# Attention heads: scores from two-term keys and queries, probabilities turned in place

## The chip, the cores and the metric

The kernel runs on one core of a Trainium2 chip. The metric is the device time of one execution in microseconds; the median of three runs counts. TensorE (PE in the profile) multiplies matrices, VectorE (DVE) and ScalarE (ACT) work element by element, GpSimd (POOL) issues most of the small transfers (DMAs), SyncE (SP) the loads of the weights. Each engine works through its own instructions in order and waits on semaphores for the others.

## The reference

One decoder layer on 512 tokens of width 2048, all in float32. What the change touches is the forgetting attention, 8 heads of 128:

```
c = cumsum(log_sigmoid(f_logit + b_f))           # per head, over tokens
logits = q @ k.T * 128**-0.5 + c[:, None] - c[None, :]
logits = where(causal, logits, -inf)
p = softmax(logits)                              # 512 x 512, lower triangle
attn = p @ v
```

Before it stands one input projection (conv B, C, V, Q, K, V, forget logits, gates); behind it gated sums, an output projection and a squared-ReLU MLP.

## The kernel before

Large products are fp32r products of two terms: a value is split into a high part (`high_of`, a rounding copy on ACT, L111) and a low part (`low_of`, a subtraction on DVE, L114), and high x high, high x low and low x high are added in PSUM (L171, L175, L177). A 512x512 block product is done as seven products of quarters (a Strassen scheme, `Group`), whose operand sums are DVE subtractions of 128x2048 (L128). One quarter product is 32 + 16 products of 256 columns. The weight quarters are loaded into four buffers `x`, their parts into two buffers each, `th` and `tl`.

The attention heads have no stage of their own. They run between the products of the first four conv groups (the input projection's columns for the convolution): `beat` counts these products, and at counts held in `places` a step of a head is put between them: `meet(h)` at 76 + 156 h (mix of head h-1, fetch of its values, scores of head h), `shares` 52 later, `turn_of(h)` 112 later. On TensorE these steps keep the order in which they are written (`sure`); on the other engines a list scheduler sets the order from its own estimates.

A head's steps: `terms` fetches a row of the running sums into the first 512 columns of `p` in all partitions; `values` fetches the values `vv`; `scores` puts a mask into PSUM (a bf16 identity times a bf16 mask, L911), adds fp32 products of queries and keys (L916), reduces each of the four row blocks with the terms into `p` (DVE, L929, which also finds the extreme of each row) and takes exponentials (ACT, L935); `shares` divides by the row sums (L941, L944); `turns` transposes ten 128x128 blocks on TensorE (L952) and copies them to `pT` (DVE L954, L955, ACT L956); `mixed` multiplies them with the values (L963, ten fp32 products of 128 columns), copies the sums to `pT` (ACT, L965) and stores them to `a_d` (POOL, L966). Row block qi holds (qi+1) x 128 columns; in `p` it begins at column 896, 1024, 512, 0 for qi = 0 to 3 (`AT`). Each of `p`, `pT`, `vv`, `kT` and `qT` has one buffer.

Of the kernel before, what the change touches and what calls it, by code (L numbers as in the profile page):

```python
# [24 lines left out]
NH = AW // P  # L25
DFF = 4 * D
EPS = 1e-6
NEG = -1.0e30
# [17 lines left out]
def tile_hybrid_block(ctx: ExitStack, tc, x, g_mix, w_in, b_f, b_gate, conv_w, w_conv_out,  # L46
                      w_attn_out, w_mix_out, g_mlp, w_ff1, w_ff2, g_final, out):
    nc = tc.nc
    x, out = x[0], out[0]
# [3 lines left out]
    const = ctx.enter_context(tc.tile_pool(name="const", bufs=1))  # L53
# [9 lines left out]
    def bank(i, name):  # L63
        return psum.tile([P, S], F32, tag=f"p{i}", name=name)
# [51 lines left out]
    def split(src, hi, lo):  # L116
        return high_of(src, hi), low_of(src, hi, lo)
# [426 lines left out]
    class Quarters:  # L544
# [162 lines left out]
    both = pair(6, F32, "junk")  # L707
# [131 lines left out]
    def at(tag, name=None, shape=None, bufs=1):  # L839
        return pb.tile(shape or [P, S], F32, tag=tag, name=name or tag, bufs=bufs)  # L840
# [7 lines left out]
    nc.vector.scalar_tensor_tensor(out=lf, in0=fl, scalar=0.0, in1=fa, op0=ALU.min, op1=ALU.subtract)  # L848
    AT = (P * 7, P * 8, P * 4, 0)
    BANK = ((7, 3 * P), (6, 0), (7, 0), (5, 0))  # L850

    def rows_of(tag, name, w=1280):
        return at(tag, name, [P, 1280])[:, :w]

    raw_ut = rows_of("pT", "ut", S)
# [3 lines left out]
    ut = pb.tile([P, 1280], F32R, tag="p", name="utr")[:, :S]  # L859
    nc.scalar.activation(out=ut, in_=raw_ut, func=AF.Copy)  # L860
    lf2 = pb.tile([P, 2, NT, NH], F32R, tag="vv", name="lf2")
    lf2 = lf2[:, 0], lf2[:, 1]
    split(lf, *lf2)
    identb = const.tile([P, P], BF16, name="identb")
    nc.vector.tensor_copy(identb, ident)
    maskb = const.tile([P, P], BF16, name="maskb")
    nc.gpsimd.memset(maskb, 0.0)
    nc.gpsimd.affine_select(out=maskb, in_=maskb, compare_op=ALU.is_ge, fill=NEG, base=0,
                            pattern=[[-1, P]], channel_multiplier=1)
    cn = const.tile([P, NT, NH], F32, name="cn")  # L870

    def sure(i):
        return tc.keep_in_program_order(i)

    def running():

        pc = bank(4, "pc")
        for t in range(NT):
            for e in range(2):
                sure(nc.tensor.matmul(pc[:NH, t * P:], lf2[e][:, t, :], ut[:, :S - t * P], start=(t == 0 and e == 0),  # L880
                                      stop=(t == NT - 1 and e == 1)))
        ncT = at("pT", "ncT", [P, 1280])[:NH, :S]
        nc.vector.tensor_scalar(out=ncT, in0=pc[:NH, :], scalar1=-1.0, scalar2=None, op0=ALU.mult)
        nc.gpsimd.dma_start(out=c_d, in_=ncT)
        return ncT

    class Head:


        def __init__(self, h):  # L890
            self.h = h
            self.kT, self.qT = at("kT"), at("qT")
            nc.gpsimd.dma_start(out=self.kT, in_=kq_d[0, h])
            nc.gpsimd.dma_start(out=self.qT, in_=kq_d[1, h])

        def terms(self):
            self.p = at("p", shape=[P, 1280])
            nc.gpsimd.dma_start(out=self.p[:, :S], in_=c_d[self.h:self.h + 1, :].to_broadcast([P, S]))

        def values(self):  # L900
# [4 lines left out]
        def scores(self):  # L905
            p, h = self.p, self.h
            at_bank = {i: bank(i, "sc") for i in (7, 6, 5)}
            sc = [at_bank[i][:, c:c + (qi + 1) * P] for qi, (i, c) in enumerate(BANK)]

            def masked(o, n):  # L910
                sure(nc.tensor.matmul(o.rearrange("p (n k) -> p n k", n=n), identb,  # L911
                                      maskb.unsqueeze(1).to_broadcast([P, n, P]), start=True, stop=False,
                                      skip_group_check=True))
# [12 lines left out]
            least, bias, total, back = (stat.tile([P, NT], F32, tag=n, name=n) for n in ("nm", "bias", "sm", "rs"))  # L926
            for qi in range(NT):
                n = (qi + 1) * P
                nc.vector.tensor_tensor_reduce(out=p[:, AT[qi]:AT[qi] + n], in0=sc[qi], in1=p[:, :n], scale=-1.0,  # L929
                                               scalar=-NEG, op0=ALU.add, op1=ALU.min, accum_out=least[:, qi:qi + 1])  # L930
            sub(bias, least, cn[:, :, h])
            add(bias, bias, cn[:, :, h])
            for qi in range(NT):
                o = p[:, AT[qi]:AT[qi] + (qi + 1) * P]
                nc.scalar.activation(out=o, in_=o, func=AF.Exp, bias=bias[:, qi:qi + 1], scale=-1.0,  # L935
                                     accum_out=total[:, qi:qi + 1])
            self.total, self.back = total, back
# [6 lines left out]
                nc.vector.tensor_scalar(out=o, in0=o, scalar1=back[:, qi:qi + 1], scalar2=None, op0=ALU.mult)  # L944

        def turns(self):
            self.pT = at("pT", shape=[P, 1280])
            at_bank = {i: bank(i, "tp") for i in (7, 6, 5)}
            for qi in (0, 2, 1, 3):
                i, c = BANK[qi]  # L950
                for ki in range(qi + 1):
                    sure(nc.tensor.transpose(at_bank[i][:, c + ki * P:c + (ki + 1) * P],  # L952
                                             self.p[:, AT[qi] + ki * P:AT[qi] + (ki + 1) * P], ident))
            nc.vector.tensor_copy(self.pT[:, S:2 * S], at_bank[7])  # L954
            nc.vector.tensor_copy(self.pT[:, 2 * S:], at_bank[6][:, :2 * P])  # L955
            nc.scalar.activation(out=self.pT[:, :S], in_=at_bank[5], func=AF.Copy)  # L956
# [12 lines left out]
    heads8, places = {}, {}  # L969

    def begin_terms():
        ncT = running()
        heads8[0].terms()
        heads8[0].values()

        def columns():
            pcn = bank(5, "pcn")
            for t in range(NT):
                sure(nc.tensor.transpose(pcn[:, t * NH:(t + 1) * NH], ncT[:, t * P:(t + 1) * P], ident[:NH, :NH]))
            nc.vector.tensor_scalar(out=cn.rearrange("p t h -> p (t h)"), in0=pcn[:, :NT * NH], scalar1=-1.0,  # L980
                                    scalar2=None, op0=ALU.mult)
        places[FIRST - 20] = columns

    def meet(h):

        def step():
            if h > 0:
                heads8[h - 1].mixed()
                if h < NH:
                    heads8[h].values()  # L990
            if h < NH:
                heads8[h].scores()
                if h + 1 < NH:
                    heads8[h + 1] = Head(h + 1)
        return step

    def turn_of(h):

        def step():
            heads8[h].turns()  # L1000
            if h + 1 < NH:
                heads8[h + 1].terms()
        return step

    for h in range(NH + 1):
        places[FIRST + PERIOD * h] = meet(h)
        if h < NH:
            places[FIRST + PERIOD * h + SHARE] = lambda h=h: heads8[h].shares()
            places[FIRST + PERIOD * h + TURN] = turn_of(h)
    places[32] = begin_terms  # L1010
    heads8[0] = Head(0)
    made = [0]

    def step_at(n):
# [81 lines left out]
    n = 0  # L1096
# [784 lines left out]
```

## Time and profile before

| | us |
|---|---|
| median of 3 runs | 2405.5 (2404.98 to 2408.44) |
| profiled execution | 2406.2 |
| its span, first to last instruction | 2404.5 |
| PE busy | 2389.2 |
| DVE busy | 2030.0 |
| ACT busy | 1205.1 |

The span is what the core's instructions cover; the execution's time has 1.7 us around it. The views used below: the page's list of engines; a table of stretches; lists of waits; the chain of waits, followed back from the last instruction, each piece being what the next one was released by; timelines of an engine; the transfers with their time from issue to landing. Records of TensorE overlap, since products are pipelined: the pace is read from one start to the next, or from the chain.

### The profile page before, as it was taken

The numbers are of one execution on the slowest core, as the hardware profiler recorded it, in microseconds if no ns is written. First come the engines' busy times: TensorE is split into PE (matmuls) and PEld (weight loads), VectorE is DVE, ScalarE is ACT, GpSimd is POOL, SyncE is SP. The second block draws the span as 40 slices with busy tenths as digits, with TensorE's granted clock in tenths as the row PEclk, the third lists the DMA queues.
The fourth block names the chain that finished last, engine by engine and source line by source line (L and its number), as shares of the span: only waits on it lengthen the run. The fifth ranks groups of instructions, "written<-read, shape, count | busy, mean of one in ns | idle before, by whom it ended". The sixth has DMA issues, their size and how long they took to land.

```text
span 2404.5 us, 41377 instructions
## 1 busy us (share of the span) xinstructions
PE 2389.2 (99%) x17778; PEld 2256.0 (94%) x17778; DVE 2030.0 (84%) x1684; ACT 1205.1 (50%) x1240; POOL 288.2 (12%) x459
## 2 busy tenths in 40 slices
PE   9999999999999999999999999999999999999998
PEld 9999999999999999899999999999998888888886
DVE  7987777789888778889988989888897888889898
ACT  7443444445545534456656666665665333333334
POOL 1100111121111102012200000000001001100000
PEclk9999999999999999999999999999999999999999
DMA  8665544565565756566856565665688557665662
GB/s 277 183 191 154 168 145 150 156 204 159 172 207 177 259 191 209 161 210 223 316 192 231 183 232 181 214 213 197 233 303 293 169 196 253 219 217 183 231 231 101
DMA packets 282599, 491.98 MB, mean 205 GB/s; under 512 B 11820, under 2 KB 192136, under 8 KB 282032
## 3 DMA queue, kind: packets, MB, share of 16 engines
q1 hardware_dynamic: 229552, 277.96, 36.5%
q0 software_dynamic: 50096, 206.39, 23.4%
q10 hardware_dynamic: 2768, 4.99, 0.6%
q8 instruction: 139, 2.28, 0.4%
q14 instruction: 44, 0.36, 0.0%
HBM read 379.70 MB, written 109.07 MB: 203 GB/s over the span
## 4 chain that ended last, share of the span: by engine, by line
PE 91%; issue 3%; DVE 3%; ACT 1%; DMA 1%; POOL 1%; SPq 0%; DVEq 0%; POOLq 0%; ACTq 0%
PE a L171 6%; PE a L175 6%; PE a L177 6%; PE d L171 5%; PE d L175 5%; PE a L199 5%; PE a L197 5%; PE a L195 5%; PE d L177 5%; PE c L171 4%; PE c L177 4%; PE c L175 4%; PE d L195 3%; PE d L197 3%; PE d L199 3%
## 5 line engine op out<-in xcount | busy, mean ns | idle before, releaser
L111 ACT ACTIVATE th<-x 128x2048 fp32r<-128x2048 f32 (+1 forms) x280 | 537.0, 1918 | 479.9 <-DVE x L128 162.7
L114 DVE TENSOR_TENSOR tl<-x,th 128x2048 fp32r<-128x2048 f32 (+2 forms) x282 | 639.3, 2273 | 151.9 <-ACT th L111 147.7
L128 DVE TENSOR_TENSOR x<-x,x 128x2048 f32<-128x2048 f32 (+1 forms) x160 | 365.9, 2287 | 23.0 <-DMA x<-in_w_in_dram 18.4
L111 ACT ACTIVATE th<-y 128x2048 fp32r<-128x2048 f32 (+1 forms) x109 | 185.4, 1701 | 273.2 <-PE a L197 138.8
L114 DVE TENSOR_TENSOR tl<-y,th 128x2048 fp32r<-128x2048 f32 (+1 forms) x109 | 219.3, 2013 | 26.7 <-ACT th L111 26.3
L197 PE MATMUL a<-th,us 128*128 128x512 f32 x512 | 199.2, 389 | 0.0
L195 PE MATMUL a<-th,us 128*128 128x512 f32 x512 | 199.2, 389 | 0.0
L171 PE MATMUL c<-S,th 128*128 128x256 f32 x848 | 195.7, 277 | 0.0
L175 PE MATMUL c<-S,th 128*128 128x256 f32 x848 | 195.5, 276 | 0.0
L171 PE MATMUL a<-S,th 128*128 128x256 f32 x784 | 181.5, 278 | 1.0 <-ACT o L269 1.0
L175 PE MATMUL a<-S,th 128*128 128x256 f32 x784 | 180.3, 276 | 0.0
L175 PEld LDWEIGHTS c<-S,th 128*128 128x128 f32 x848 | 159.3, 188 | 0.0
L171 PEld LDWEIGHTS c<-S,th 128*128 128x128 f32 x848 | 159.3, 188 | 0.0
L171 PEld LDWEIGHTS a<-S,th 128*128 128x128 f32 x784 | 147.2, 188 | 1.4 <-ACT o L269 1.2
L175 PEld LDWEIGHTS a<-S,th 128*128 128x128 f32 x784 | 147.3, 188 | 0.2 <-issue 0.2
L199 PE MATMUL a<-tl,us 128*128 128x512 f32 x512 | 136.7, 389 | 0.0
L171 PE MATMUL a<-A,th 128*128 128x256 f32 x544 | 126.6, 278 | 0.0
L171 PE MATMUL b<-A,th 128*128 128x256 f32 x544 | 126.3, 278 | 0.0
L171 PE MATMUL d<-S,th 128*128 128x256 f32 x544 | 126.0, 277 | 0.0
L175 PE MATMUL a<-A,th 128*128 128x256 f32 x544 | 125.5, 276 | 0.0
L171 PE MATMUL d<-A,th 128*128 128x256 f32 x544 | 125.4, 276 | 0.0
L175 PE MATMUL b<-A,th 128*128 128x256 f32 x544 | 125.4, 276 | 0.0
(409 smaller groups left out, 6012.2 us busy)
## 6 DMA issues: line engine op xcount, KB each, us to landing
x<-in_w_in_dram SPq DMA_DIRECT2D x86, 1024.0 KB, 5.9
y<-in_w_ff_dram SPq DMA_DIRECT2D x64, 1024.0 KB, 7.8
x<-in_w_ff_dram SPq DMA_DIRECT2D x60, 1024.0 KB, 8.3
us<-s_d POOLq DMA_DIRECT2D x44, 1024.0 KB, 9.0
s_d<-rh POOLq DMA_DIRECT2D x32, 896.0 KB, 5.3
s_d<-r POOLq DMA_DIRECT2D x32, 896.0 KB, 5.7
x<-in_w_mix_out_dram SPq DMA_DIRECT2D x17, 1024.0 KB, 6.7
g_d<-o POOLq DMA_DIRECT2D x32, 256.0 KB, 3.2
```

The source lines that it names most:

```text
L111: return tied(nc.scalar.activation(out=hi, in_=src, func=AF.Copy))
L114: return tied(nc.vector.tensor_tensor(out=lo, in0=src, in1=hi.bitcast(F32), op=ALU.subtract))
L128: return nc.vector.tensor_tensor(out=out, in0=a, in1=b, op=ALU.subtract)
L171: i = nc.tensor.matmul(o, hi[:, q, js], Sh, start=first and q == 0 and j == 0, stop=False, skip_group_check=True)
L175: nc.tensor.matmul(o, hi[:, q, js], Sl, start=False, stop=False, skip_group_check=True)
L177: i = nc.tensor.matmul(o, lo[:, q, js], Sh, start=False, stop=q == nq - 1, skip_group_check=True)
L195: tied(nc.tensor.matmul(o, Sh, hi[:, q, :], start=begin and q == 0, stop=False, skip_group_check=True))
L197: tied(nc.tensor.matmul(o, Sl, hi[:, q, :], start=False, stop=False, skip_group_check=True))
L199: tied(nc.tensor.matmul(o, Sh, lo[:, q, :], start=False, stop=q == nq - 1, skip_group_check=True))
```

## The change

Keys and queries are split into two terms (`cut`, at counts 80 and 96 of the period before), and scores are three fp32r products a row block instead of one in fp32 (which has two records). The mask is made of fp32r tiles. The transposed probabilities are laid out by keys and go back into `p` itself, so that the mix is four fp32 products of 512, 384, 256 and 128 columns instead of ten of 128; `pT` is gone, and `p` is one tile for all heads. Its terms for the next head are therefore fetched by `mixed`, behind the products, and no longer by `turn_of`; the head's output is copied to columns 512 to 1023 of `p` and stored from there. The fetch of the values is issued behind this store. Shares come at 60 instead of 52, and the reductions are written in the order 0, 2, 1, 3.

```diff
-    identb = const.tile([P, P], BF16, name="identb")
...
+    raw_mask = lead[:, 2 * S:2 * S + P]
...
         def __init__(self, h):
-            self.h = h
-            self.kT, self.qT = at("kT"), at("qT")
-            nc.gpsimd.dma_start(out=self.kT, in_=kq_d[0, h])
-            nc.gpsimd.dma_start(out=self.qT, in_=kq_d[1, h])
+            self.h, self.k2, self.q2 = h, [], []
+            for j, two in enumerate((self.k2, self.q2)):
+                for e in ("high", "low"):
+                    two.append(pb.tile([P, S], F32R, tag=f"{'kq'[j]}{e}", name=f"{'kq'[j]}T"))
+                nc.gpsimd.dma_start(out=two[1].bitcast(F32), in_=kq_d[j, h])
+
+        def cut(self, j):
+
+            hi, lo = (self.k2, self.q2)[j]
+            split(lo.bitcast(F32), hi, lo)
 
         def terms(self):
-            self.p = at("p", shape=[P, 1280])
+            self.p = at("p", shape=[P, 1280]) if self.h == 0 else heads8[self.h - 1].p
...
             def product(qi):
-                sure(nc.tensor.matmul(sc[qi], self.qT[:, qi * P:(qi + 1) * P], self.kT[:, :(qi + 1) * P], start=False,
-                                      stop=True, skip_group_check=True))
+                (kh, kl), (qh, ql) = self.k2, self.q2
+                ks, qs = slice((qi + 1) * P), slice(qi * P, (qi + 1) * P)
+                for q, k in ((qh, kh), (qh, kl), (ql, kh)):
+                    sure(nc.tensor.matmul(sc[qi], q[:, qs], k[:, ks], start=False, stop=q is ql, skip_group_check=True))
...
-            for qi in range(NT):
+            for qi in (0, 2, 1, 3):
...
         def mixed(self):
-            o = bank(4, "o")
-            for qi in range(NT):
-                for ki in range(qi + 1):
-                    a = AT[qi] + ki * P
-                    sure(nc.tensor.matmul(o[:, qi * P:(qi + 1) * P], self.vv[:, ki, :], self.pT[:, a:a + P],
-                                          start=(ki == 0), stop=(ki == qi)))
-            nc.scalar.activation(out=self.pT[:, :S], in_=o, func=AF.Copy)
-            nc.gpsimd.dma_start(out=a_d[self.h], in_=self.pT[:, :S])
+            p, o = self.p, bank(4, "o")
+            for ki in range(NT):
+                n, a = S - ki * P, TURNED[ki]
+                sure(nc.tensor.matmul(o[:, ki * P:], self.vv[:, ki, :], p[:, a:a + n], start=(ki == 0),
+                                      stop=(ki == NT - 1)))
+            if self.h + 1 < NH:
+                heads8[self.h + 1].terms()
+            nc.scalar.activation(out=p[:, S:2 * S], in_=o, func=AF.Copy)
+            self.stored = nc.gpsimd.dma_start(out=a_d[self.h], in_=p[:, S:2 * S])
...
-    FIRST, PERIOD, SHARE, TURN = 76, 156, 52, 112
+    FIRST, PERIOD, SHARE, TURN = 76, 156, 60, 112
...
         def step():
             heads8[h].turns()
-            if h + 1 < NH:
-                heads8[h + 1].terms()
```

How this moves instructions on DVE is seen at the hand-over to head 1. `sc` are the scores, `nm` the rows' extremes, `tl` and `th` low and high parts of a conv quarter, `x` such quarters, `o` a product's sums; `DMASW` are semaphores of transfers issued by POOL, `DMAHW` of those by SP, the others are engines. The reductions, before:

```order
L131 TENSOR_TENSOR o<-c,o 128x512 [waits DMASW2_49,Activation_49]
L929 ISA p,nm<-sc,p 128x128 [waits DMASW4_49,DVE_49,PE_49]
L929 ISA nm 128x1
L929 ISA p,nm<-sc,p 128x384
L929 ISA nm 128x1
L929 ISA p,nm<-sc,p 128x256 [waits PE_49]
```

The same place after the change:

```order
L131 TENSOR_TENSOR o<-c,o 128x512 [waits Activation_49]
L938 ISA p,nm<-sc,p 128x256 [waits DMASW4_49,DVE_49,PE_49]
L938 ISA nm 128x1
L938 ISA p,nm<-sc,p 128x128 [waits DMASW5_49,Activation_49]
L938 ISA nm 128x1
L938 ISA p,nm<-sc,p 128x384
L938 ISA nm 128x1
L114 TENSOR_TENSOR tl<-x_2819,th 128x2048 [waits PE_49]
```

The 256-wide reduction now stands first and waits for the terms (DMASW4); the 128-wide one behind it waits for a second transfer (DMASW5, the store of the head before) and for ACT; a low part of the conv product has moved ahead of the last reduction. The rest of this hand-over on DVE, from the bias to the shares, before:

```order
L128 TENSOR_TENSOR bias<-nm,cn 128x4 [waits DVE_49]
L131 TENSOR_TENSOR bias<-bias,cn 128x4 [waits DVE_49]
L114 TENSOR_TENSOR tl<-x_2820,th 128x2048 [waits PE_49,Activation_49]
L131 TENSOR_TENSOR o<-a,o 128x512 [waits Activation_49]
L941 RECIPROCAL rs<-sm 128x4 [waits Activation_49]
L944 TENSOR_SCALAR p<-p,rs 128x128 [waits DVE_49]
L944 TENSOR_SCALAR p<-p,rs 128x256
L944 TENSOR_SCALAR p<-p,rs 128x384
L944 TENSOR_SCALAR p<-p,rs 128x512
L114 TENSOR_TENSOR tl<-x_3337,th 128x2048 [waits DMAHW7_49,PE_49,Activation_49]
L131 TENSOR_TENSOR o<-a,o 128x512 [waits Activation_49]
L128 TENSOR_TENSOR x_3337<-x_3513,x_3337 128x2048 [waits DMAHW1_49,DVE_49]
```

And after, from the last reduction to the first share:

```order
L938 ISA p,nm<-sc,p 128x512 [waits DVE_49]
L938 ISA nm 128x1
L131 TENSOR_TENSOR o<-a,o 128x512 [waits Activation_49]
L128 TENSOR_TENSOR bias<-nm,cn 128x4 [waits DVE_49]
L114 TENSOR_TENSOR kT<-kT 128x512 [waits DMASW7_49,Activation_49]
L131 TENSOR_TENSOR bias<-bias,cn 128x4 [waits DVE_49]
L114 TENSOR_TENSOR qT<-qT 128x512 [waits DMASW0_49,Activation_49]
L114 TENSOR_TENSOR tl<-x_3362,th 128x2048 [waits DMAHW7_49,PE_49,Activation_49]
L950 RECIPROCAL rs<-sm 128x4 [waits Activation_49]
L128 TENSOR_TENSOR x_3362<-x_3540,x_3362 128x2048 [waits DMAHW1_49,DVE_49]
L131 TENSOR_TENSOR o<-a,o 128x512 [waits Activation_49]
L953 TENSOR_SCALAR p<-p,rs 128x128 [waits DVE_49]
```

Two cuts have come in, and the low part, the subtraction of operands and the addition that stood behind the shares now stand ahead of them. On POOL the transfers around the same hand-over, before:

```order
L898 DMA p<-c_d 128x512 [waits DMASW4_49,DVE_49,PE_49]
L903 DMA vv<-v_d 128x4x128 [waits DMASW6_49,DMASW5_49,PE_49]
L966 DMA a_d<-pT 128x512 [waits Activation_49]
L893 DMA kT<-kq_d 128x512 [waits DMASW1_49,PE_49]
L894 DMA qT<-kq_d 128x512 [waits DMASW2_49,DMASW0_49]
```

And after:

```order
L905 DMA p<-c_d 128x512 [waits DMASW4_49,PE_49]
L977 DMA a_d<-p 128x512 [waits DMASW5_49,Activation_49]
L910 DMA vv<-v_d 128x4x128 [waits DMASW6_49,PE_49]
L896 DMA kT<-kq_d 128x512 [waits PE_49]
L896 DMA qT<-kq_d 128x512 [waits DMASW0_49,DVE_49,PE_49]
```

The terms' place in this list is the same, but what they wait for on TensorE is now a product of the mix instead of the transposes, and the store has moved ahead of the values.

## Rows read from the trace of the kernel before

**Rows 1.** The page's first part: busy us (share of the span) and instructions.

```profile
PE 2389.2 (99%) x17778; PEld 2256.0 (94%) x17778; DVE 2030.0 (84%) x1684; ACT 1205.1 (50%) x1240; POOL 288.2 (12%) x459
```

**Rows 2.** Stretches: start:end, length, busy us per engine, clock, DMA.

```profile
255.00:460.00 205.00, 205.00 (x1704) 196.36 (x1703) 152.53 (x207) 91.67 (x127) 36.39 (x58) 1.00 0.50 153
```

**Rows 3.** Chain of waits at the hand-over to head 1: start, us, what.

```profile
286.61 2.23 PE o L963 x20
288.95 0.87 PE sc L916 x4
289.88 0.49 PE sc L916 x2
290.42 0.91 PE sc L916 x2
...
295.88 1.81 PE c L177 x16
```

**Rows 4.** Timeline of TensorE at a 192-column product: start, us, engine, line.

```profile
555.35 0.19 PEld L1077 LDWEIGHTS spare<-S,th 128*128 128x128 f32 x1
555.46 0.25 PE L1077 MATMUL spare<-S,th 128*128 128x192 f32 x1
555.46 0.19 PEld L171 LDWEIGHTS a<-S,th 128*128 128x128 f32 x1
555.54 0.30 PE L171 MATMUL a<-S,th 128*128 128x256 f32 x1
555.57 0.19 PEld L175 LDWEIGHTS a<-S,th 128*128 128x128 f32 x1
```

**Rows 5.** Chain of waits, the running sums (512, 384, 256, 128 columns, twice each).

```profile
258.03 1.17 PE pc L880 x8
```

**Rows 6.** Instruction groups by form: count, busy us, mean ns, idle before.

```profile
L114 DVE TENSOR_TENSOR M<-merged,M 128x512 fp32r<-128x512 f32 x23 | 15.6, 686 | 1.9 <-ACT M L111 1.8
```

**Rows 7.** Timeline of POOL before and at the hand-over to head 1.

```profile
281.90 0.56 POOL L898 DMA_DIRECT2D p<-c_d  x1 [10.42 <-PE tp L952]
...
289.88 0.55 POOL L966 DMA_DIRECT2D a_d<-pT  x1
```

**Rows 8.** DMA issues, 279 to 302 us: count, KB each, us to landing.

```profile
a_d<-pT POOLq DMA_DIRECT2D x1, 256.0 KB, 3.6
```

**Rows 9.** All eight stores of L966, landing.

```profile
DMA to landing us min/median/max: 2.4/3.6/6.7
```

**Rows 10.** Timeline of DVE at the hand-over to head 1.

```profile
289.86 0.29 DVE L929 CUSTOM_DVE_ANT_0 p<-sc,p 128x128 f32<-128x128 f32 x1 [4.74 <-PE sc L916]
290.07 0.55 DVE L929 CUSTOM_DVE_ANT_0 p<-sc,p 128x384 f32<-128x384 f32 x1
...
291.37 0.69 DVE L929 CUSTOM_DVE_ANT_0 p<-sc,p 128x512 f32<-128x512 f32 x1 [0.39 <-PE sc L916]
292.11 0.17 DVE L128 TENSOR_TENSOR bias<-nm,cn 128x4 f32<-128x4 f32 x1
...
292.39 2.29 DVE L114 TENSOR_TENSOR tl<-x,th 128x2048 fp32r<-128x2048 f32 x1
...
295.40 1.45 DVE L944 TENSOR_SCALAR p<-p,rs 128x128 f32<-128x128 f32 x4
...
300.68 4.61 DVE L128 TENSOR_TENSOR x<-x,x 128x2048 f32<-128x2048 f32 x2
```

**Rows 11.** Timeline of TensorE: mix of head 0, transposes of head 1.

```profile
286.45 2.39 PE L963 MATMUL o<-pT,vv 128*128 128x128 f32 x20
...
303.88 1.25 PE L952 MATMUL tp<-ident,p 128*128 128x128 f32 x10
```

**Rows 12.** Head 4: last copy on DVE's timeline, next mix in the chain.

```profile
379.16 0.41 DVE L955 COPY pT<-tp 128x256 f32<-128x256 f32 x1
...
382.10 2.23 PE o L963 x20
```

**Rows 13.** Chain of waits, sixteen 256-column products at another time.

```profile
307.97 1.88 PE a L177 x16
```

More of the change, by code (lines that the diff above doesn't have):

```diff
@@ L850, in tile_hybrid_block @@
     BANK = ((7, 3 * P), (6, 0), (7, 0), (5, 0))
+    TURNED, TURNED_BANK = (0, P * 4, P * 8, P * 7), ((5, 0), (7, 0), (6, 0), (7, 3 * P))
     def rows_of(tag, name, w=1280):
         return at(tag, name, [P, 1280])[:, :w]
-    raw_ut = rows_of("pT", "ut", S)
+    lead = rows_of("p", "lead")
+    raw_ut = lead[:, S:2 * S]
     nc.gpsimd.memset(raw_ut, 1.0)
@@ L858, in tile_hybrid_block @@
                             pattern=[[1, P]], channel_multiplier=-1)
-    ut = pb.tile([P, 1280], F32R, tag="p", name="utr")[:, :S]
+    ut = pb.tile([P, S], F32R, tag="vv", name="utr")
     nc.scalar.activation(out=ut, in_=raw_ut, func=AF.Copy)
-    lf2 = pb.tile([P, 2, NT, NH], F32R, tag="vv", name="lf2")
-    lf2 = lf2[:, 0], lf2[:, 1]
+    lf2 = pb.tile([P, 2, P], F32R, tag="both", name="lf2")
+    lf2 = tuple(lf2[:, e, :NT * NH].rearrange("p (t h) -> p t h", t=NT) for e in range(2))
     split(lf, *lf2)
-    identb = const.tile([P, P], BF16, name="identb")
[L865 to L868, printed above, removed]
+    raw_mask = lead[:, 2 * S:2 * S + P]
+    nc.gpsimd.memset(raw_mask, 0.0)
+    nc.gpsimd.affine_select(out=raw_mask, in_=raw_mask, compare_op=ALU.is_ge, fill=NEG, base=0,
                             pattern=[[-1, P]], channel_multiplier=1)
+    mask2 = []
     cn = const.tile([P, NT, NH], F32, name="cn")
@@ L881, in running @@
                                       stop=(t == NT - 1 and e == 1)))
-        ncT = at("pT", "ncT", [P, 1280])[:NH, :S]
+        ncT = lead[:NH, S:2 * S]
         nc.vector.tensor_scalar(out=ncT, in0=pc[:NH, :], scalar1=-1.0, scalar2=None, op0=ALU.mult)
@@ L910, in masked @@
             def masked(o, n):
-                sure(nc.tensor.matmul(o.rearrange("p (n k) -> p n k", n=n), identb,
-                                      maskb.unsqueeze(1).to_broadcast([P, n, P]), start=True, stop=False,
+                sure(nc.tensor.matmul(o.rearrange("p (n k) -> p n k", n=n), mask2[0][:, 0],
+                                      mask2[0][:, 1].unsqueeze(1).to_broadcast([P, n, P]), start=True, stop=False,
                                       skip_group_check=True))
             def product(qi):
-                sure(nc.tensor.matmul(sc[qi], self.qT[:, qi * P:(qi + 1) * P], self.kT[:, :(qi + 1) * P], start=False,
-                                      stop=True, skip_group_check=True))
+                (kh, kl), (qh, ql) = self.k2, self.q2
+                ks, qs = slice((qi + 1) * P), slice(qi * P, (qi + 1) * P)
+                for q, k in ((qh, kh), (qh, kl), (ql, kh)):
+                    sure(nc.tensor.matmul(sc[qi], q[:, qs], k[:, ks], start=False, stop=q is ql, skip_group_check=True))
             masked(at_bank[7][:, 2 * P:], 2)
@@ L946, in turns @@
         def turns(self):
-            self.pT = at("pT", shape=[P, 1280])
+            p = self.p
             at_bank = {i: bank(i, "tp") for i in (7, 6, 5)}
             for qi in (0, 2, 1, 3):
-                i, c = BANK[qi]
                 for ki in range(qi + 1):
[L952 to L956, printed above, removed]
-        def mixed(self):
-            o = bank(4, "o")
-            for qi in range(NT):
-                for ki in range(qi + 1):
-                    a = AT[qi] + ki * P
-                    sure(nc.tensor.matmul(o[:, qi * P:(qi + 1) * P], self.vv[:, ki, :], self.pT[:, a:a + P],
-                                          start=(ki == 0), stop=(ki == qi)))
-            nc.scalar.activation(out=self.pT[:, :S], in_=o, func=AF.Copy)
-            nc.gpsimd.dma_start(out=a_d[self.h], in_=self.pT[:, :S])
-    FIRST, PERIOD, SHARE, TURN = 76, 156, 52, 112
+                    i, c = TURNED_BANK[ki]
+                    c += (qi - ki) * P
+                    sure(nc.tensor.transpose(at_bank[i][:, c:c + P], p[:, AT[qi] + ki * P:AT[qi] + (ki + 1) * P], ident))
+            nc.vector.tensor_copy(p[:, S:2 * S], at_bank[7])
+            nc.vector.tensor_copy(p[:, 2 * S:], at_bank[6][:, :2 * P])
+            nc.scalar.activation(out=p[:, :S], in_=at_bank[5], func=AF.Copy)
+        def mixed(self):
+            p, o = self.p, bank(4, "o")
[8 more added lines that the diff above has]
+    FIRST, PERIOD, SHARE, TURN = 76, 156, 60, 112
     heads8, places = {}, {}
@@ L972, in begin_terms @@
         ncT = running()
+        mask2.append(pb.tile([P, 2, P], F32R, tag="both", name="both"))
+        for e, src in enumerate((ident, raw_mask)):
+            nc.scalar.activation(out=mask2[0][:, e], in_=src, func=AF.Copy)
         heads8[0].terms()
@@ L989, in step @@
                 if h < NH:
-                    heads8[h].values()
+                    with tc.issue_after(heads8[h - 1].stored.ins):
+                        heads8[h].values()
             if h < NH:
@@ L1009, in tile_hybrid_block @@
             places[FIRST + PERIOD * h + TURN] = turn_of(h)
+        if h + 1 < NH:
+            for j in range(2):
+                places[FIRST + PERIOD * h + 80 + 16 * j] = lambda h=h, j=j: heads8[h + 1].cut(j)
     places[32] = begin_terms
     heads8[0] = Head(0)
+    for j in range(2):
+        places[8 + 8 * j] = lambda j=j: heads8[0].cut(j)
     made = [0]
```

## The prediction

> **What bounds the kernel now.** I read the views in this order. The page's first part: TensorE is busy for 99% of the span [rows 1]. The stretch table: the eight attention heads lie between 255 and 460 us, between the conv products, and there TensorE is busy in all 205.00 us, DVE in 152.53, ACT in 91.67 [rows 2]. The chain of waits runs there from one TensorE instruction to the next: mix, scores, conv product [rows 3]. So every microsecond taken from the head's TensorE work comes off the total, and every microsecond by which DVE, ACT or a transfer makes TensorE wait goes on top of it. A head's work comes as a block at a hand-over: the mix of head h-1 (L963), at once the scores of head h (L911, L916), later the transposes (L952); a period of 23 to 24 us lies between two hand-overs.
>
> **TensorE, scores.** Now, from the end of the mix (286.61 + 2.23 = 288.84) to the next conv product (291.33, the end of 290.42 + 0.91), a head's masks and scores take 2.49 us [rows 3]. They are four fp32 products of 128, 256, 384 and 512 columns (two records each) and three bf16 masks. The change makes of them twelve fp32r products and three fp32r masks, 15 instructions, each with a new 128x128 weight. Prices: sixteen 256-column fp32r products take 1.81 us, 0.113 each [rows 3]; for 384 and 512 I take 1.5 and 2 times that, 0.170 and 0.226. The price of a 128-column one is not in the trace with a full weight. Below it is bounded by the running sums, whose weights are only 8 columns wide: eight in 1.17 us, 2560 columns, 0.46 ns a column, so 0.058 for 128 [rows 5]. Above it is bounded by the weight loads: around a 192-column product they start at 555.35, 555.46 and 555.57, 0.11 apart, though that product itself lasts only until 555.54, when the next begins, 0.08 later [rows 4]; the one after that starts 0.14 later in its turn. Loads of full weights thus come every 0.113 us whatever is streamed. I take 0.113, since rows 4 have the weights of the new products and rows 5 have not. A head then costs one 256-column mask and two of 128 (3 x 0.113), 128-column products (3 x 0.113), 256 (3 x 0.113), 384 (3 x 0.170) and 512 (3 x 0.226): 2.21 us. That is 0.28 less than 2.49, for eight heads **-2.3 us**. With 0.058 it would be 5 x 0.055 = 0.28 more a head, -4.5 in all; nothing gained (0) is the other end, if changing the kind of operand costs as much as the bf16 mask does now (the 0.49 for 256 columns and 0.91 for 512, against 0.87 for 128 and 384 together, hold such pauses).
>
> The Trainium skill ("TensorE: Matmul & The Clock Gate", Back-to-back issue gap) gives an isolated gap of columns/2.4 + 2.5 ns, 56 ns for 128 columns. By it the scores would gain some 4.6 us. The 0.11 between loads in rows 4 speaks against it for a stream with a new fp32 weight each time.
>
> **TensorE, mix.** Ten products of 128 columns become four of 512, 384, 256 and 128, all fp32: 1280 columns as before, 2.23 us now [rows 3]. The scores of before are the same four widths in fp32: 0.87 + 0.49 + 0.91 = 2.27, with the pauses behind the masks in them. I take 2.18, -0.05 a head, **-0.4 us** (from -0.8 to +0.3). The ten transposes go to other columns and cost the same.
>
> **The cuts.** Each head gets two high copies on ACT and two subtractions on DVE of 128x512; such a subtraction takes 0.69 us [rows 6]. Eight heads make 11 us on DVE, of its 52 idle ones, and about as much on ACT, of its 113 [rows 2]. Cost 0 where idle time covers it; they count below, where they stand before something late. The mask's two copies and memsets run beside conv products: 0.
>
> **The wait that is added.** Now the row of the next head's terms is fetched into p right after the transposes (281.90), 8 us before it is read, and the head's output goes out of pT at 289.88 while DVE already reduces scores at 289.86 [rows 7, 10]. After the change p is the only tile. Terms are fetched when the first mix product has read p, and the output leaves from p columns 512 to 1023, which the reductions of rows 128 and 384 wide write. By the order of DVE the 128-wide reduction waits for that store (its second transfer semaphore), and behind it on DVE stand everything else, the conv products' low parts too.
>
> I follow the worst hand-over, that to head 1, in time from the start of the mix, T = 286.45 [rows 11]. The store is issued at 289.88, T+3.4 [rows 7], say T+3.3, as it stands ahead of the values' fetch now. Stores here land 3.6 us after issue [rows 8], so the 128-wide reduction starts at T+7.0, where it now starts at T+3.4 (289.86) [rows 10]. From there I add up DVE as the order has it: reductions 128 and 384 (0.29 + 0.55), a low part (2.29), reduction 512 (0.69), an addition (0.69), bias, key cut, bias, query cut (0.17 + 0.69 + 0.17 + 0.69), a low part (2.29), reciprocal (0.2), a subtraction of operands (2.3, half of 4.61), an addition (0.69) and the four shares (1.45) [rows 6, 10]. That is 13.2 us; records that follow each other overlap by 0.08 (289.86 + 0.29 against 290.07), so 12.3 to run: the shares are done at T+19.3. The transposes stand at 303.88, T+17.4 [rows 11], 17.1 after the savings, and would end at T+18.2; their last four need the last share and end at about T+19.9. TensorE stands for **+1.7 us**. Two things make this hand-over the worst: the subtraction of 2.3 us stands ahead of the shares here and at no other one, and a low part stands between the reductions (so at head 5 too, where I get T+17 for the shares, just in time).
>
> At the other hand-overs reductions end near T+8.3, exponentials near T+11 and shares at T+12.6 to 13.5, four ahead of the transposes. What is late next are the copies out of the transposes, which the next mix reads. At head 4 they end at 379.57 (379.16 + 0.41), 2.5 before the mix at 382.10 [rows 12]; there DVE comes some 1.6 later behind the wait and the cuts, so about 1 us is left. Cost 0, but not by much. Where stores landed in 6.7 [rows 9], up to 3 us more are to be covered; at heads 3 and 7, where that may happen, the low part ahead of the exponentials uses the wait.
>
> The Trainium skill ("DMA: Bandwidth & Descriptors", Anatomy of one DMA) puts a DMA issued by GpSimd at 2.0 us plus size over 436 GB/s, 2.6 for these 256 KB. Then 1.0 of the 1.7 us would not arise. The 3.6 of rows 8 decides for me.
>
> **Sum.** -2.3 - 0.4 + 1.7 = -1.0 us against the profiled execution, 2406.2 (span 2404.5 and 1.7 around it), that is 2405.2. The median of the runs is 0.7 lower, 2405.5, so I predict 2404.5.
>
> **Rivals.**
> 1. The wait is hidden everywhere (store in 2.6, or DVE ahead). The gain stands alone: 2405.5 - 2.7 = 2402.8. For: TensorE found its operands ready throughout the stretch [rows 2]. Against: the sum for head 1.
> 2. Cheap 128-column products besides (0.058, the page's gap): -4.5 - 0.4, with little or no wait, 2400.6. Against: rows 4.
> 3. Slower: the store sets the pace at every hand-over. If it lands in 5.7 rather than 3.6, the other six pass their 1 us by about 1.1 to 1.5 each and head 1 pays 3.8: 8 + 3.8 - 2.7 = +9, 2414.5. It decides from a landing of about 4.6 us on; rows 9 have 6.7 as the longest, and five transfers now leave within 4 us, the terms among them.
> 4. The pace of conv products. Sixteen take 1.81 us at one time and 1.88 at another [rows 3, 13], at the same granted clock [rows 2], and what sets it I cannot read. The slower pace holds over some 76 us of the stretch. If the new blocks end it, 3.9% of 76, -2.9: 2401.6; if it holds to the end, 3.9% of some 130 more, +5: 2409.5.
>
> **How the numbers follow.** Chances: forecast 0.45, rival 1 0.17, rival 2 0.08, rival 3 0.18, rival 4 0.06 each way. 0.2% is 4.8 us, about what a measurement tells from no change: faster means below 2400.7, slower above 2410.3. Faster: rival 2 (0.08), the lower halves of rivals 1 and 4 (0.07): 0.15. Slower: rival 3 (0.18) and a little of rival 4: 0.20. Same: 0.65. The range reaches from rival 2 to just beyond rival 4, 2400 to 2411, and leaves out most of rival 3 and a little below. The forecast's own range is 2402 to 2407.
>
> **What would show it.** Scores and masks of a head take 2.2 us on TensorE, loads 0.11 apart, the mix 2.2. DVE stands before the 128-wide reduction, until about 7 us after the mix began. TensorE waits once for more than 1 us, at the transposes of head 1, for the shares. It would be wrong if the 128-column products start 0.06 apart, if several transposes or mixes wait, or if the conv products between change their pace.

## The result, and the profile after

The changed kernel takes 2413.92 us (median of 8 runs, 2412.39 to 2415.26), the kernel before, on the same chip, 2407.11 (8 runs): a ratio of 1.003, 95% interval 1.0021 to 1.0039. It is 6.8 us slower; forecast were 2404.5 and a range that ended at 2411. The profiled execution took 2413.94, its span of 2412.2 is 7.7 longer than before's.

The page's first part and three stretches of the changed kernel (start:end, length, busy us per engine, granted clock, DMA share, GB/s) answer to [rows 1, 2]:

```profile
PE 2390.1 (99%) x17714; PEld 2256.8 (94%) x17714; DVE 2038.7 (85%) x1699; ACT 1212.7 (50%) x1258; POOL 287.3 (12%) x459
```

```profile
255.00:460.00 205.00, 199.68 (x1600) 191.54 (x1600) 154.70 (x218) 98.41 (x145) 33.58 (x54) 0.99 0.48 151
386.00:396.00 10.00, 10.00 (x74) 9.28 (x73) 3.30 (x7) 2.45 (x3) 2.91 (x5) 1.00 0.92 285
399.78:403.30 3.52, 3.52 (x17) 3.52 (x18) 3.52 (x6) 2.86 (x10) 0.00 (x0) 0.53 0.96 299
```

The last two stretches belong to head 5 below. TensorE now stands for 5.3 us of the 205 in which it never stood. To find where, I took the same conv products in both traces and compared their starts. Most of the shift arises in the places of the first four rows:

| place (time in the kernel before) | shift added, us |
| --- | --- |
| 145 to 165 us, long before the first head | +1.5 a wait, +0.65 slower pace of products |
| head 1's transposes | +1.38 |
| head 4's mix | +1.36 |
| behind the scores of head 5 | +3.38 (3.00 of it a wait), +1.73 products at half pace |
| everywhere else up to 437 us (the heads' gain, changes of pace) | -2.1 |
| sum at 437 us | +7.9 |

From there to the end small steps of both signs leave 7.7.

**At 145 us.** ScalarE's timeline of the changed kernel (start, us, engine, line, tile, and in brackets the idle time before and what ended it):

```profile
137.63 0.63 ACT L111 ACTIVATE qT<-qT 128x512 fp32r<-128x512 f32 x1 [5.64 <-DMA qT<-kq_d]
...
144.17 0.63 ACT L111 ACTIVATE kT<-kT 128x512 fp32r<-128x512 f32 x1 [4.10 <-DMA kT<-kq_d]
```

Head 0's cuts, whose results are needed 120 us later, stand in the queue between the high parts of the conv groups, before their loads have landed. Behind them the group's work is late, and TensorE's timeline has

```profile
149.59 0.39 PE L171 MATMUL c<-S,th 128*128 128x256 f32 x1 [1.36 <-DVE o L286]
```

**Head 1.** DVE's timeline answers to [rows 10], TensorE's to [rows 11]; T, the start of the mix, is now 288.53:

```profile
294.98 0.42 DVE L938 CUSTOM_DVE_ANT_0 p<-sc,p 128x256 f32<-128x256 f32 x1 [5.90 <-DMA p<-c_d]
295.65 0.29 DVE L938 CUSTOM_DVE_ANT_0 p<-sc,p 128x128 f32<-128x128 f32 x1 [0.23 <-DMA a_d<-p]
...
303.80 2.29 DVE L128 TENSOR_TENSOR x<-x,x 128x2048 f32<-128x2048 f32 x1
306.01 0.68 DVE L131 TENSOR_TENSOR o<-a,o 128x512 f32<-128x512 f32 x1
306.61 0.54 DVE L953 TENSOR_SCALAR p<-p,rs 128x128 f32<-128x128 f32 x2
```

```profile
307.04 0.30 PE L963 MATMUL tp<-ident,p 128*128 128x128 f32 x1 [0.74 <-DVE p L953]
```

The 128-wide reduction starts at T+7.1 (forecast T+7.0), and the transposes wait for the shares, as forecast. But nearly all of the waiting on DVE, 5.90 us, ends with the landing of the terms, not of the store, which lands 0.7 us behind them. (In the kernel before, DVE stood 4.74 us here for the scores [rows 10].)

**Head 4.** ScalarE's timeline, then TensorE's [rows 12]:

```profile
383.06 1.92 ACT L111 ACTIVATE th<-x 128x2048 fp32r<-128x2048 f32 x1 [5.11 <-DVE x L128]
384.88 0.57 ACT L966 ACTIVATE p<-tp 128x512 f32<-128x512 f32 x1
```

```profile
385.51 2.42 PE L972 MATMUL o<-p,vv 128*128 128x512 f32 x8 [1.38 <-ACT p L966]
```

The copy that the mix waits for is ScalarE's, behind a high part that waited for DVE. I had followed DVE's copies only.

**Head 5.** The chain of waits (start, us, what):

```profile
388.86 6.54 DMA a_d<-p
...
395.54 0.29 DVE p L938
...
396.31 2.20 DVE tl L114
398.51 0.60 DVE p L938
...
399.12 0.61 DVE o L131
...
400.44 0.21 PE c L171
400.66 0.21 PE c L175
```

and, with the idle times, from the timelines of DVE and TensorE:

```profile
395.54 0.29 DVE L938 CUSTOM_DVE_ANT_0 p<-sc,p 128x128 f32<-128x128 f32 x1 [4.40 <-DMA a_d<-p]
...
399.78 0.44 PE L171 MATMUL c<-S,th 128*128 128x256 f32 x1 [3.00 <-DVE o L131]
```

The store takes 6.54 us to land while the DMA engines are busy for 0.92 of the stretch 386 to 396. DVE stands 4.40 for it, and the addition L131, which empties bank c (the PSUM bank that the next conv products write), stands behind the reductions: TensorE is idle for 3.00 us. Its next products then start 0.21 apart rather than 0.11, at a granted clock of 0.53 in the stretch above, about the lower of its two levels (1.2 of 2.4 GHz).

**The gain.** TensorE's timeline of head 4's scores, behind the mix of head 3, answers to [rows 3]:

```profile
360.72 2.32 PE L972 MATMUL o<-p,vv 128*128 128x512 f32 x8
362.80 0.36 PE L918 MATMUL sc<-both 128*128 128x256 f32 x1
363.00 1.03 PE L926 MATMUL sc<-kT,qT 128*128 128x128 f32 x6
363.86 0.22 PE L918 MATMUL sc<-both 128*128 128x128 f32 x1
363.92 0.57 PE L926 MATMUL sc<-kT,qT 128*128 128x256 f32 x3
364.33 0.22 PE L918 MATMUL sc<-both 128*128 128x128 f32 x1
364.39 0.92 PE L926 MATMUL sc<-kT,qT 128*128 128x512 f32 x3
365.15 0.28 PE L171 MATMUL a<-A,th 128*128 128x256 f32 x1
```

From the start of the mix to that of the scores it takes 2.08 us (before, 2.23), from there to the next conv product 2.35 (before, 2.49 [rows 3]): 0.3 us gained per head, as forecast (0.33), though with other shares.

### The profile page after: what moved, and what is told of

Read it like the earlier page. It is cut to its first block, busy times and chain, and to the rows that moved or that the text cites. A ratio compares the mean times of both kernels' runs of the same rounds, so it can differ in the third digit from the quotient of the medians.

```text
span 2412.2 us, 41291 instructions
## 1 busy us (share of the span) xinstructions
PE 2390.1 (99%) x17714; PEld 2256.8 (94%) x17714; DVE 2038.7 (85%) x1699; ACT 1212.7 (50%) x1258; POOL 287.3 (12%) x459
## 4 chain that ended last, share of the span: by engine, by line
PE 80%; issue 6%; DVE 4%; DMA 2%; POOL 1%; ACT 1%; POOLq 0%; DVEq 0%; ACTq 0%
PE a L171 6%; PE a L175 5%; PE a L177 5%; PE a L199 5%; PE a L197 5%; PE a L195 5%; PE d L171 5%; PE d L175 5%; PE d L177 5%; PE c L171 4%; PE c L177 4%; PE c L175 3%; PE d L195 3%; PE d L197 3%; PE d L199 3%
## 5 line engine op out<-in xcount | busy, mean ns | idle before, releaser
L128 DVE TENSOR_TENSOR x<-x,x 128x2048 f32<-128x2048 f32 (+1 forms) x160 | 365.7, 2286 | 20.7 <-DMA x<-in_w_in_dram 18.4
```

The costliest lines, as they stand in the source:

```text
L128: return nc.vector.tensor_tensor(out=out, in0=a, in1=b, op=ALU.subtract)
```

## The experiments

The theory after this comparison: what the heads lose is the wait for the store's landing; head 0's cuts are a second, separate loss. The rivals: the two-term scores and their cuts themselves; the terms, fetched behind the mix. Ratios are to the kernel before on the same chip (medians of 2406.5 to 2407.1 us). Differences between runs of different chips, those to the changed kernel among them, carry these 0.6 us besides. In the code, "..." stands for lines left out.

**own_place.** The head's output leaves from the value tile, which the mix has finished with; the next values are fetched behind the next keys and queries.

```
-            nc.scalar.activation(out=p[:, S:2 * S], in_=o, func=AF.Copy)
-            self.stored = nc.gpsimd.dma_start(out=a_d[self.h], in_=p[:, S:2 * S])
+            out = self.vv.rearrange("p t c -> p (t c)")
+            nc.scalar.activation(out=out, in_=o, func=AF.Copy)
+            self.stored = nc.gpsimd.dma_start(out=a_d[self.h], in_=out)
...
```

> Theory (the store): the changed kernel lost its time where the next head's first reductions waited for the landing of the store of the head's output, because both use one part of p: 1.4 us at head 1's transposes, 1.4 us at head 4's mix, 3.4 us at the hand-over to head 5 and 1.7 us of slower products behind it. Here the output is copied into the value tile, which the mix has just finished with, and stored from there; only the load of the next values waits for it. The terms are still fetched behind the mix. Expected: the loss of 3 to 5 us at head 5 goes, some of the 2.8 us of heads 1 and 4 too, while the head 0 cuts still cost 2 us: 2407 to 2409 us, 5 to 7 below the changed kernel's 2413.9. Rival (the scores' products or the terms are what costs): no more than 2 us below it, 2412 or above.

2407.58 us, ratio 1.0002 (0.9994 to 1.0011), 6.3 below the changed kernel. In its trace the losses at heads 1, 4 and 5 are gone, that at 148 us is not (0.9 us), and a new one of 1.25 us appears at 442 us. As the theory has it, but for the new loss.

**late_cuts.** Head 0's cuts later in the program, and kept in program order.

```
...
-        places[8 + 8 * j] = lambda j=j: heads8[0].cut(j)
+        places[40 + 8 * j] = lambda j=j: heads8[0].cut(j)
```

> Theory (head 0's cuts): the two cuts of head 0's keys and queries stood among the conv groups on ScalarE and VectorE before their loads had landed, held both engines for 4 to 5.6 us at 137 to 144 us and so made the products of 145 to 165 us about 2 us late. Here those four instructions are issued some 24 us later in program order, nothing else moves. Expected: the shift of 1.5 us at 148 us and of 2.1 us at 165 us goes to 0, the rest stays: 2411.5 to 2412.5 us. Rival (the shift at 148 us has another cause, or is made up later): 2413 to 2415 us.

2413.39 us, ratio 1.0027 (1.0016 to 1.0038): in the rival's range, and by time alone not to be told from the changed kernel. In the trace the step at 148 us is gone; that execution lost 1.7 us to a slower pace of the products between 31 and 77 us instead, which no edit touches, and 1.7 more at 1074 to 1080 us.

**own_late.** Both edits.

> Both edits. If the two causes are separate and their losses add up: 2405 to 2407 us, within 0.2% of the kernel before, and with the gain of 0.3 us per head left over perhaps 2404. Rival (scores and mix on the array themselves cost time): 2409 us or more.

2405.58 us, ratio 0.9997 (0.9989 to 1.0006), 2.0 below own_place. The trace gains steadily, 3.07 us at 437 us, and then loses 1.34 at the hand-over to head 7. DVE there:

```profile
431.61 0.29 DVE L940 CUSTOM_DVE_ANT_0 p<-sc,p 128x128 f32<-128x128 f32 x1 [2.96 <-DMA p<-c_d]
...
436.34 0.18 DVE L952 RECIPROCAL rs<-sm 128x4 f32<-128x4 f32 x1 [2.36 <-ACT p L946]
436.55 1.28 DVE L955 TENSOR_SCALAR p<-p,rs 128x128 f32<-128x128 f32 x4
438.15 2.29 DVE L114 TENSOR_TENSOR tl<-x,th 128x2048 fp32r<-128x2048 f32 x1 [0.32 <-ACT th L111]
440.36 0.68 DVE L131 TENSOR_TENSOR o<-c,o 128x512 f32<-128x512 f32 x1
```

With no store to wait for, DVE still stands 2.96 us for the terms, and again bank c is emptied too late.

**in_place_only.** The changed kernel with the scores of the kernel before.

```
...
-                for q, k in ((qh, kh), (qh, kl), (ql, kh)):
-                    sure(nc.tensor.matmul(sc[qi], q[:, qs], k[:, ks], start=False, stop=q is ql, skip_group_check=True))
+                sure(nc.tensor.matmul(sc[qi], self.qT[:, qi * P:(qi + 1) * P], self.kT[:, :(qi + 1) * P], start=False,
+                                      stop=True, skip_group_check=True))
...
```

> The changed kernel with the scores of the kernel before (plain fp32 keys and queries, bf16 mask, no cuts), but the probabilities turned in place, the terms fetched behind the mix, the output stored from p and the mix by keys. Theory (the store): the waits at heads 1, 4 or 5 are still there, without any cut: 2409 to 2413 us, 3 to 7 above the kernel before. Rival (two-term scores and their cuts cost the time): 2404 to 2407 us, as the kernel before.

2410.93 us, ratio 1.0017 (1.0007 to 1.0026): in the theory's range, but only half for its reason. The trace has one costly wait for the store, at the hand-over to head 7 (2.2 us), and at heads 1, 4 and 5 none that costs (at head 5 DVE stands 3.94 for it):

```profile
439.92 0.29 DVE L931 CUSTOM_DVE_ANT_0 p<-sc,p 128x128 f32<-128x128 f32 x1 [4.49 <-DMA a_d<-p]
```

Another 2.6 us are lost at 1074 to 1080 us, far from the heads.

**late_landing.** Three more stores ahead of the real one. They also add traffic and put off the fetch of the values behind them, so the run tests a later landing together with these.

```
...
+            for e in range(3):
+                nc.gpsimd.dma_start(out=spare_d[e, self.h], in_=p[:, S:2 * S])
             self.stored = nc.gpsimd.dma_start(out=a_d[self.h], in_=p[:, S:2 * S])
```

> The changed kernel, with three more stores of the head's output (to a spare place in HBM) queued on GpSimd ahead of the real one, so that p is held longer: each takes 0.55 us to issue, so the last landing comes some 1.7 us or more later at every hand-over. Theory (the store's landing sets when DVE goes on): the wait before the 128-wide reduction grows by about that at each of the seven hand-overs, and TensorE pays it where nothing is left to cover it (heads 1, 4 and 5 at least): 4 to 9 us more, 2418 to 2423 us. Rival (the cuts' time on the engines is what is late, the landing is covered): 2413 to 2416 us.

2423.62 us, ratio 1.0069 (1.0055 to 1.0082): 9.7 above the changed kernel, a little more than expected. It is paid at other places: against the changed kernel's trace, the slower products behind each stand included, +2.9 at head 1, +7.0 at head 3, +5.4 at the hand-over to head 7, and -4.8 at head 5, where DVE now stands only 0.95 us for the store. DVE at heads 3 and 7:

```profile
353.21 0.29 DVE L939 CUSTOM_DVE_ANT_0 p<-sc,p 128x128 f32<-128x128 f32 x1 [5.54 <-DMA a_d<-p]
...
455.28 0.29 DVE L939 CUSTOM_DVE_ANT_0 p<-sc,p 128x128 f32<-128x128 f32 x1 [6.96 <-DMA a_d<-p]
```

So a late landing can cost at hand-overs where the changed kernel paid nothing, and which ones they are changes with the order of the transfers.

**mix_only.** The kernel before with the layout by keys and the wide mix alone.

```
...
+            for ki in range(NT):
+                n, a = S - ki * P, TURNED[ki]
+                sure(nc.tensor.matmul(o[:, ki * P:], self.vv[:, ki, :], self.pT[:, a:a + n], start=(ki == 0),
+                                      stop=(ki == NT - 1)))
...
```

> The kernel before with one part of the change alone: probabilities turned into columns by keys and a mix of four wide products instead of ten of 128 columns, with the second tile, the early terms and the fp32 scores as before. Theory: this part gains 0.08 to 0.16 us a head and brings no wait: 2405 to 2407 us, not to be told from the kernel before. Rival (the new mix itself disturbs the products): 2409 us or more.

2407.36 us, ratio 1.0003 (0.9994 to 1.0012): not to be told from the kernel before, as expected, though 0.4 us beyond the expected range. From mix to scores 2.15 us instead of 2.23, and no wait at any head. Its trace too loses 3.1 us at 1074 to 1080 us.

**plain_scores_own_place.** in_place_only with the edit of own_place.

> The fourth corner of two scores by two places of the output: plain fp32 scores without cuts as in in_place_only, and the output stored from the value tile as in own_place. Theory (the store): 2405 to 2407 us, 4 below in_place_only, and within 1 to 2 of own_late, since two-term scores gain only 0.15 us a head. Rival (the wait costs only beside the cuts): no lower than in_place_only, 2409 to 2411 us.

2410.41 us, ratio 1.0018 (1.0009 to 1.0027): a miss. With plain scores the place of the output gains nothing (in_place_only has 1.0017 on its chip), not 4 us. DVE at head 5:

```profile
389.17 0.29 DVE L931 CUSTOM_DVE_ANT_0 p<-sc,p 128x128 f32<-128x128 f32 x1 [7.00 <-DMA p<-c_d]
```

The terms landed 6.2 us after their issue; that cost 1.6 us, another 0.9 were lost at head 7, and 3.1 at 1074 to 1080 us again. So the store was not the only landing that counts.

**mix_ahead.** own_late with the mix ten products before the next scores and the transposes six earlier.

```
...
-    FIRST, PERIOD, SHARE, TURN = 76, 156, 60, 112
...
+    FIRST, PERIOD, SHARE, TURN = 76, 156, 60, 106
...
+            places[FIRST + PERIOD * h - 10] = lambda h=h: heads8[h - 1].mixed()
...
```

> own_late with the mix ten conv products ahead of the next head's scores and the transposes six ahead of where they were, so that the terms, fetched behind the mix's first product, land about 1.1 us earlier before the reductions. own_late's trace lost 1.3 us at 441 us where DVE had stood 2.96 us for the terms. Theory: that goes, 2403.5 to 2405 us. Rival (the copies of the turned probabilities are then late for the mix): 2406 to 2409 us.

2412.58 us, ratio 1.0025 (1.0015 to 1.0035): a miss, above the rival's range too. The mix of head 1 stopped for a copy, as the rival had it, and a later group waited longer, for ScalarE. TensorE:

```profile
311.26 1.56 PE L974 MATMUL o<-p,vv 128*128 128x384 f32 x6 [1.12 <-DVE p L966]
...
402.47 0.38 PE L171 MATMUL d<-A,th 128*128 128x256 f32 x1 [2.83 <-ACT th L111]
```

What that left open (the terms' share) the last two runs take up.

**early_row.** own_late, with the terms in a tile of their own, fetched with the transposes as before the change.

```
...
+            self.row = otile([P, S], "row")
+            nc.gpsimd.dma_start(out=self.row, in_=c_d[self.h:self.h + 1, :].to_broadcast([P, S]))
...
-                nc.vector.tensor_tensor_reduce(out=p[:, AT[qi]:AT[qi] + n], in0=sc[qi], in1=p[:, :n], scale=-1.0,
+                nc.vector.tensor_tensor_reduce(out=p[:, AT[qi]:AT[qi] + n], in0=sc[qi], in1=self.row[:, :n], scale=-1.0,
...
```

> own_late with the next head's terms in a tile of their own (one of the five output tiles of the products' groups, which rotate), fetched with the transposes as in the kernel before, so that neither the store nor the terms are waited for by a reduction. Theory (both landings together are the loss): the 1.3 us that own_late's trace still lost at 441 us goes, the gain of 0.3 us a head stays: 2403 to 2405 us, below the kernel before. Rival (an output tile less makes the products' groups wait, or the terms were never the cause): 2406 us or more.

2402.52 us, ratio 0.9982 (0.9973 to 0.9991): 4.2 below the kernel before, 11.4 below the changed one, the fastest here and 0.5 below the expected range. TensorE never stands between 255 and 460 us:

```profile
255.00:460.00 205.00, 205.00 (x1667) 196.82 (x1666) 162.09 (x223) 101.76 (x147) 38.82 (x64) 1.00 0.50 157
```

**early_row_alone.** The changed kernel with that edit only.

> The changed kernel with the terms alone in a tile of their own and fetched early; the output is still stored from p, and head 0's cuts stay where they are. Theory (the store is the later of the two landings at the hand-overs that cost, since it is issued 1.3 us or more after the terms): the loss at heads 1, 4 and 5 stays for the most part, 2410 to 2413 us. Rival (the terms were what was late): 2406 to 2408 us, as in own_place.

2404.11 us, ratio 0.9989 (0.998 to 0.9998), 9.8 below the changed kernel: a miss, and the rival's number bettered. The store is still waited for, at five hand-overs, but behind less. DVE at head 5:

```profile
385.00 0.42 DVE L939 CUSTOM_DVE_ANT_0 p<-sc,row 128x256 f32<-128x256 f32 x1 [3.48 <-PE sc L927]
...
385.93 0.69 DVE L939 CUSTOM_DVE_ANT_0 p<-sc,row 128x512 f32<-128x512 f32 x1 [0.50 <-PE sc L927]
...
387.75 0.29 DVE L939 CUSTOM_DVE_ANT_0 p<-sc,row 128x128 f32<-128x128 f32 x1 [1.11 <-DMA a_d<-p]
```

The 256- and 512-wide reductions, which write where the store does not read, now run while the store is under way (in the changed kernel the 512-wide one came last, behind a low part), and the wait is 1.11 us instead of 4.40. Of the losses up to 460 us only 0.8 us at 148 us are left.

DMA issues around head 5 (count, KB each, us to landing) of the changed kernel, then of early_row_alone:

```profile
x<-in_w_in_dram SPq DMA_DIRECT2D x2, 1024.0 KB, 6.7
p<-c_d POOLq DMA_DIRECT2D x1, 256.0 KB, 3.6
a_d<-p POOLq DMA_DIRECT2D x1, 256.0 KB, 6.5
```

```profile
x<-in_w_in_dram SPq DMA_DIRECT2D x2, 1024.0 KB, 6.0
a_d<-p POOLq DMA_DIRECT2D x1, 256.0 KB, 3.2
```

The weight fetch next to the store differs too. SyncE's timeline of the changed kernel, then of early_row_alone:

```profile
388.43 0.37 SPq L235 DMA_DIRECT2D x<-in_w_in_dram  x1
```

```profile
381.55 0.37 SPq L235 DMA_DIRECT2D x<-in_w_in_dram  x1
```

In the changed kernel it is issued 0.4 us ahead of the store (388.86), in early_row_alone 2.9 ahead (384.45), in the kernel before 3.6 ahead. Each time it was released by the same low part on DVE. In the changed kernel that ends 2.9 us behind the start of the mix (385.51), in the kernel before 0.3 ahead of it (382.10 [rows 12]).

**What follows.** After the change a head's reductions follow two transfers that begin only with the mix: the terms (mix, fetch, landing) and the store (mix, copy, store, landing). In the changed kernel DVE stood 20.7 us for the first at the seven hand-overs and 10.2 for the second; not all of it is new, since in the kernel before it stood 14.6 there for the scores. With the two-term scores, taking either away removes the losses at heads 1, 4 and 5 (own_place, early_row_alone); taking the terms' away is worth 3.5 us more. Of these, 1.25 are the loss at head 7 that own_place has and early_row_alone has not, 0.5 come earlier; the rest lies behind the heads, 1.1 of it at 1114 us, and its cause is open. Both edits also let the reductions and the work around them come in another order on DVE; how much of their gain is that order and how much the landing I cannot separate.

## Why the prediction was wrong, step by step

- **Scores, -0.28 a head.** Right in sign, half in size: 2.49 became 2.35, -0.14. The mis-sized terms are the first mask, 0.20 (362.80 to 363.00) where I had 0.11, and the 384-column products, 0.58 (363.28 to 363.86) where I had 0.51; the two other masks and the 256- and 512-column products were 0.05 more together, the 128-column products 0.06 less. Narrower stretches of the same timeline split the rows:

```profile
362.76 0.28 PE L972 MATMUL o<-p,vv 128*128 128x128 f32 x1
...
363.06 0.61 PE L926 MATMUL sc<-kT,qT 128*128 128x128 f32 x3
363.28 0.57 PE L926 MATMUL sc<-kT,qT 128*128 128x384 f32 x2
```

  The second of the 128-column products starts 0.06 behind the first, the three take 0.28 (363.00 to 363.28), so the other two 0.11 each: the price lay between my bounds, near the upper one, and I had 0.34. The Trainium skill's isolated gap of 56 ns ("TensorE: Matmul & The Clock Gate", Back-to-back issue gap) is met, about, by that first gap alone; the same section says that it is too low for a stream of weight loads and narrow products.
- **Mix, -0.05 a head.** Under-sized: -0.15 (2.23 to 2.08), of which mix_only shows 0.08 for the layout. The other 0.07 are probably a matter of the border: the first mask starts 0.04 behind the last product of the mix, in mix_only 0.11 behind it, and its 0.20 are the longer for it. Both together gave the 0.3 a head that the sum had.
- **"The cuts ... Cost 0 where idle time covers it."** Failed for head 0: +1.5 us. I had added up their durations against idle time and not looked where the order puts head 0's: they wait for loads, and a wait of 5.64 us costs more than a copy of 0.63. late_cuts and own_late, in whose traces the step is gone, show it; the times alone show it weakly (0.5 and 2.0 us).
- **The wait at head 1, +1.7.** Held: +1.38, with the 128-wide reduction at T+7.1. What the sum did not have is that the terms land no earlier: fetched at about T+1.5, they took 5.0. I had counted "the terms among them" only as company for the store.
- **"At the other hand-overs ... Cost 0, but not by much."** This is the step that failed most: heads 4 and 5 cost 1.36, 3.38 and 1.73. At head 4 the late copy was ScalarE's. At head 5 the store landed not in 3.6 us but in 6.5, and I had followed the shares there ("just in time") and not the addition that empties bank c, which stands in the same queue.
- **Landing, 3.6 (at most 6.7).** The median was again 3.6, but the changed kernel's eight stores landed in 2.4 to 7.1 us. One number for seven hand-overs was the error: each one has its own, and it goes with the weight fetch beside it (below). The 3.6 of rows 8 is of a store issued 5.3 us behind a fetch, the 6.7 of rows 9 of one issued 1.0 behind. The Trainium skill's price ("DMA: Bandwidth & Descriptors", Anatomy of one DMA), by which I estimate 2.6 us for such a transfer, is near the shortest seen here, 2.4.
- **What was not in the sum:** the half pace behind a long stand of TensorE, +1.73 us.
- **Rival 3** gave the time (2414.5) but not the way: the store did not pace every hand-over. At head 3 it landed in 7.1 us, and DVE stood 2.79 for it at no cost to TensorE; TensorE paid at head 1's transposes, at head 4's mix and behind head 5's scores. **Rival 4** was there with 0.65 us.

The long landing at head 5 can be read further in the traces, though no run varied it alone. The eleven traces without the three added stores have 88 such stores. The 18 that were issued within 1.6 us behind a weight fetch of 1 MB landed in 5.7 to 7.9 us, the 62 issued 2.9 us or more behind one in 2.3 to 4.8, the 8 between in 3.7 to 6.8. At head 5 of the changed kernel DVE, late by its waits and cuts, released the fetch 0.4 us ahead of the store, and the landing made DVE later still: the prediction had no term for what a late DVE does to the transfers.

What stays open: how much of the edits' gain is the order on DVE and how much the landing; and the 2.6 to 3.1 us at 1074 to 1080 us in the three runs with plain scores and the mix by keys. late_cuts, with two-term scores, lost 1.7 there, so it does not belong to plain scores alone. In mix_only TensorE waits there 1.29 for DVE and 1.62 for ScalarE:

```profile
1074.93 0.36 PE L195 MATMUL c<-th,M 128*128 128x256 f32 x1 [1.29 <-DVE o L131]
1082.44 0.39 PE L195 MATMUL d<-th,M 128*128 128x256 f32 x1 [1.62 <-ACT th L111]
```

## What to carry to other kernels

Saving a buffer by using one tile in place puts every transfer that reads or fills it into the chain: list all of them, give each the longest landing that the trace shows beside the same traffic, ask which transfers a late engine will release beside them, and follow what is queued behind the waiting instruction on every engine, above all what empties an accumulator. Small work that is "covered by idle time" is covered only if its operands are there when its turn comes in the queue. The cheapest mend here was 2 KB a partition borrowed elsewhere for the one row that could be fetched early: alone (early_row_alone) it beat both kernels, and with the two other edits (early_row) the time is 4.2 us below the kernel before.

## What the runs showed of the hardware

- After 3.00 us without work TensorE's next products, up to about 403.4 us, started 0.21 apart at a granted clock of 0.53, and from 403.6 on 0.11 to 0.12 apart; after stands of 1.36 and 1.38 us, and one of 2.83 in mix_ahead, no such stretch followed.
- The same 256 KB store, from the same queue, landed in 2.4 to 7.1 us within one execution; over eleven traces in 5.7 to 7.9 where it was issued within 1.6 us behind a 1 MB fetch, in 2.3 to 4.8 where it was 2.9 us or more behind one.
- Sixteen equal products take 1.81 or 1.88 us in stretches that change from run to run at a granted clock of 1.00; late_cuts lost 1.7 us to it at 31 to 77 us. Differences of 1 us between kernels are read from traces, place by place, not from one time.
